# RWKV-7 in a hybrid encoder step: the output product in another PSUM pair, and the inverse's join issued earlier

## The chip, the cores and the metric

The kernel runs on one core of a Trainium2 chip. The metric is the device time of one execution in microseconds (us), the median of several executions. A profile is one further execution, taken with the hardware profiler; its span runs from the first to the last instruction. TensorE is called PE here (its weight loads PEld), VectorE DVE, ScalarE ACT, GpSimd POOL and SyncE SP.

## The reference, cut to what matters

One layer of a streaming encoder works on 1024 prompt frames and 32 sample frames. After a norm and one input projection, two groups of heads read the same rows: group A is sparse attention with a top-k choice of keys, group B is RWKV-7 time mixing. Their outputs go through one output projection, then a norm and a squared-ReLU feed-forward net. The change is in group B alone. There, for each of 8 heads, a 64 x 64 state S goes through the frames:

```python
def step(S, inp):
    r_t, w_t, k_t, v_t, kk_t, b_t = inp
    s_kk = jnp.einsum('bhvk,bhk->bhv', S, kk_t)
    S = S * w_t[:, :, None, :] - s_kk[..., None] * b_t[:, :, None, :] + v_t[..., None] * k_t[:, :, None, :]
    return S, jnp.einsum('bhvk,bhk->bhv', S, r_t)

s_fin, y = lax.scan(step, wkv0.astype(f32), (tm(r_h), tm(w_h), tm(k_h), tm(v_h), tm(kk), tm(kk * a_h)))
```

After it come a norm per head, a bonus term and a gate; the result has 512 columns per frame.

## The kernel before

The program has three stages. Stage one is the input projection and the choice of keys for the attention (`phase_a`). Stage two runs the attention (`attn_all`) and RWKV (`rwkv_all`) side by side. Stage three is the output projection (`project`, `project_early`) and the feed-forward net (`phase_c`).

**RWKV in units and chunks.** The 1056 frames are five units: 0 to 3 have 256 frames in four chunks of 64 (`NC = 4`, `w = 64`), unit 4 has the 32 sample frames in one chunk. A chunk is treated at once: with G, the masked products of keys, keys-times-a and receptances (L712, L715), the recurrence inside a chunk is a triangular system whose inverse is needed. Each unit goes through these steps:

- `rwkv_front` (L596): loads, decay and normalised keys (`head_stat` L790, `lora` L626, running sums L647, `head_bcast` L806), the tiles KB and AR (L681), and for each chunk G: 16 matmuls into two PSUM tiles (L712) and two masked copies on DVE (L715). Then `lane_inverse` (L810): four transposes on DVE (L824), 62 elementwise instructions on POOL one behind the other (L829, L831), and transposes back into G (L835) and X1 (L840) on DVE. This inverts the 32 x 32 diagonal blocks.
- `rwkv_join` (L757): combines two 32 x 32 inverses into the one of 64 x 64: 64 matmuls of 32 x 32 (L768), two ACT copies (L771), 64 matmuls (L776), two ACT copies (L779) into G. Only units with `w = 64` have it.
- `rwkv_tokens` (L736), for each chunk: 8 transposes of KB with two copies on ACT (L746, L747) and 4 of v with two copies (L750, L752): the chunk's keys and values by frame, in tiles KBs and VU with three buffers.
- `rwkv_back` (L843), the chain: for each chunk the product pR (L876, L880) is copied to rh (L882), pU (L888) is copied to VU (L889, L890), pS (L895) makes the next state (L901, L902), and the output product pY, 16 matmuls L906 and 16 matmuls L910, is copied to y by ACT (L911). The next chunk's pR needs the new state, not pY.
- `rwkv_norm` (L939): the norm of y, bonus and gate (`head_bcast` L806, L950, L790, L806, L968), and the store.

**PSUM.** There are eight banks. The names that matter: `pc`, one buffer, holds pR, pU, pS and pY one after the other, and both products of the join. `pr`, two buffers (`PRB`), holds the tiles of the front, the tokens and the norm, and those of `project_early` (L1256). The attention has `pd` (two), `ptr` (two) and `po` (one). A `pr` tile is given out when the tile two before it has been read; the tiles of a name are asked for in the order in which the program was written down.

**The order of the work.** The program is written down by generators: `rwkv_all` takes one step each from the back of unit i, the norm of unit i-1 and the front of unit i+2, in turn (`while gens`, L1018), and the body (L1498) takes a step of the attention, then a step of RWKV. Which instruction an engine takes next is settled at compile time by a planner: it plays the program against its own estimate of durations and takes, of what is ready, the one written down earliest, where `high_priority` moves a step's place: the back by +300 instructions (`BOFF`), the front by -100 (`FOFF`), all of RWKV by -200 (`OFF`). On the chip each engine then works its queue in that order.

**Around the change.** `rwkv_back` begins, at L854 to L858, with the tokens of chunks 0 and 1 where they are not there yet (unit 0 alone), and with the join of its own unit. In chunk c it writes down the tokens of chunk c+2 after pY; in chunks 2 and 3 these are the tokens of the next unit's chunks 0 and 1 (L914 to L917). `lane_inverse` of unit i+2 is written down after the chain of unit i.

Of the kernel before, what the change touches and what calls it, by code (L numbers as in the profile page):

```python
# [53 lines left out]
F32 = mybir.dt.float32  # L54
# [702 lines left out]
def rwkv_join(S, ps, U):  # L757

    nc = S.nc
    X1 = U.X1.rearrange("p (c h) t -> p c h t", c=4)  # L760

    def pc():
        return ps.tile([128, 512], F32, name="pc", bufs=1).rearrange("p (a b c) -> p a b c", a=4, b=4)
    p = pc()
    for cc in range(4):
        for hp in range(4):
            for par, b in ((0, 64), (1, 0)):
                nc.tensor.matmul(p[b + 32:b + 64, cc, hp], U.G[b:b + 32, par, cc, hp, 32:64], X1[b:b + 32, cc, hp],  # L768
                                 start=True, stop=True)
    for par, b in ((0, 64), (1, 0)):  # L770
        nc.scalar.copy(X1[b + 32:b + 64], p[b + 32:b + 64])  # L771
    p = pc()
    for cc in range(4):
        for hp in range(4):
            for par, b in ((0, 64), (1, 0)):
                nc.tensor.matmul(p[b:b + 32, cc, hp], X1[b + 32:b + 64, cc, hp], U.G[b + 32:b + 64, par, cc, hp, 32:64],  # L776
                                 start=True, stop=True)
    for par, b in ((0, 64), (1, 0)):
        nc.scalar.copy(U.G[b:b + 32, par, :, :, 32:64], p[b:b + 32])  # L779
# [63 lines left out]
def rwkv_back(S, rp, ps, U, state):  # L843
    nc, I, O = S.nc, S.I, S.O
    n, NC, w, u = U.n, U.NC, U.w, U.u
    G, AR = U.G, U.AR
    y = rp.tile([128, 4, 4, 64], F32, name="y", bufs=YB)

    def pc():
        return ps.tile([128, 512], F32, name="pc", bufs=1)  # L850

    def quarter(p):
        return p[:, 0:256].rearrange("p (a b) -> p a b", a=4)
    for c in range(len(U.tok), min(NC, 2)):  # L854
        U.tok.append(rwkv_tokens(S, rp, ps, U, c))
    tok = U.tok
    if w == 64:
        rwkv_join(S, ps, U)  # L858
    yield
    st = state.get("st")  # L860
    if u == 4:
        st = rp.tile([128, 4, 64], F32, name="st", bufs=3)
        si = S.rs.tile([64, 8, 64], F32, name="tmp", bufs=2)
        nc.sync.dma_start(si, I["state_wkv"][0, 0].rearrange("h v k -> v h k"))
        p = quarter(pc())
        for hp in range(4):
            nc.tensor.transpose(p[:, hp], si[:, 2 * hp:2 * hp + 2].rearrange("p a b -> p (a b)"), S.ident[0:64, 0:64])
        nc.scalar.copy(st, p)
    for c in range(NC):
        KBs, VU = tok[c]  # L870
        first = st is None
        pR = quarter(pc())
        pairs = [(hp, par) for hp in range(4) for par in range(2)]
        for hp, par in pairs:
            a, b = PAR[par], PAR[1 - par]
            nc.tensor.matmul(pR[b, hp], G[a, par, c, hp, 0:64], VU[a, par, hp], start=(hp == 0), stop=(first and hp == 3))  # L876
        if not first:
            for hp, par in pairs:
                a, b = PAR[par], PAR[1 - par]
                nc.tensor.matmul(pR[b, hp], AR[c][a, hp, 0], st[a, hp], start=False, stop=(hp == 3))  # L880
        rh = rp.tile([128, 4, 64], F32, name="rh", bufs=2)
        nc.vector.tensor_copy(rh, pR)  # L882
        yield
        pU = quarter(pc())
        for hp in range(4):
            for par in range(2):
                b = PAR[1 - par]
                nc.tensor.matmul(pU[b, hp], G[b, par, c, hp, 0:64], rh[b, hp], start=True, stop=True)  # L888
        nc.vector.tensor_copy(VU[64:128, 0], pU[64:128])  # L889
        nc.scalar.copy(VU[0:64, 1], pU[0:64])  # L890
        yield
        pS = quarter(pc())
        for hp in range(4):
            for par in range(2):
                nc.tensor.matmul(pS[PAR[par], hp], KBs[:, par, hp], VU[:, par, hp], start=True, stop=True)  # L895
        sn = rp.tile([128, 4, 64], F32, name="st", bufs=3)
        pcb = U.PC[:, c][:, :, None].to_broadcast([128, 4, 64])
        if first:
            nc.vector.tensor_tensor(sn, pS, pcb, op=ALU.mult)
        else:  # L900
            nc.vector.tensor_tensor(sn, pS, st, op=ALU.add)  # L901
            nc.vector.tensor_tensor(sn, sn, pcb, op=ALU.mult)  # L902
        yield
        pY = quarter(pc())
        for hp, par in pairs:
            nc.tensor.matmul(pY[PAR[par], hp], VU[:, par, hp], G[:, par, c, hp, 64:128], start=(hp == 0), stop=(first and hp == 3))  # L906
        if not first:
            for hp, par in pairs:
                a = PAR[par]
                nc.tensor.matmul(pY[a, hp], st[a, hp], AR[c][a, hp, 1], start=False, stop=(hp == 3))  # L910
        nc.scalar.copy(y[:, :, c], pY)  # L911
        st = sn
        U.done = c + 1
        if c + 2 < NC:  # L914
            tok.append(rwkv_tokens(S, rp, ps, U, c + 2))
        elif U.next and TOKN and len(U.next.tok) < U.next.NC:
            U.next.tok.append(rwkv_tokens(S, rp, ps, U.next, len(U.next.tok)))  # L917
        yield
    U.done = 4
    state["st"] = st  # L920
    if u >= 3:
        p = pc()[0:64].rearrange("p (a b c) -> p a b c", a=2, b=4)
        p2 = ps.tile([128, 512], F32, name="pr", bufs=PRB)[0:64].rearrange("p (a b c) -> p a b c", a=2, b=4)
        for hp in range(4):
            nc.tensor.transpose(p[:, 0, hp], st[0:64, hp], S.ident[0:64, 0:64])
        for hp in range(4):
            nc.tensor.transpose(p2[:, 1, hp], st[64:128, hp], S.ident[64:128, 64:128])
        so = S.rs.tile([64, 4, 2, 64], F32, name="tmp", bufs=2)
        nc.scalar.copy(so[:, :, 0], p[:, 0])
        nc.scalar.copy(so[:, :, 1], p2[:, 1])  # L930
        dst = O["wkv_prompt"] if u == 3 else O["wkv_sample"]
        nc.sync.dma_start(dst.rearrange("h v k -> v h k"), so.rearrange("p a b k -> p (a b) k"))
        if u == 3:
            state["st"] = None
    U.y = y
    yield
# [35 lines left out]


YB = 2


def rwkv_all(S, order):

    state = {"st": None}
    S.units = units = [K() for _ in order]  # L980
    fronts = []
    for i, U in enumerate(units):
        U.i, U.stage, U.tok = i, 0, []
        U.next = units[i + 1] if i + 1 < len(units) else None
        fronts.append(rwkv_front(S, order[i], U, units[i - 2] if i > 1 else None))

    def ahead(i):

        for _ in fronts[i]:
            if units[i].stage == 2 and i + 1 < len(order) and PRE and i >= PREI:  # L990
                break
            yield
        else:
            return
        yield
        for _ in range(PRE):
            next(fronts[i + 1])
            yield
        yield from fronts[i]

    def norm(i):
        if i >= 0:
            yield from rwkv_norm(S, S.P[0], S.ps, units[i])
        if 0 <= i + 2 < len(order):
            rwkv_prelude(S, S.P[0], units[i + 2])
    for i in range(-2, len(order) + 1):
        gens = []
        B = front = None
        if 0 <= i < len(order):
            B = units[i]  # L1010
            gens.append(back := rwkv_back(S, S.P[0], S.ps, B, state))
        if i >= -1:
            gens.append(norm(i - 1))
            if i == 0:
                shift_rows(S, S.P[0], S.ps)
        if i + 2 < len(order):
            gens.append(front := ahead(i + 2))
        while gens:  # L1018
            for g in list(gens):
                with S.tc.high_priority(BOFF) if B and g is back else S.tc.high_priority(F0 if i == -2 else F1 if i == -1 else FOFF) if g is front else nullcontext():  # L1020
                    if next(g, 1) == 1:
                        gens.remove(g)
                yield
# [348 lines left out]
PRB = 2  # L1372
# [38 lines left out]
def body(tc, I, O, dbg=None):  # L1411
# [4 lines left out]
    with pool(name="const") as cp, pool(name="dram", space=DRAM) as dp:  # L1416
# [18 lines left out]
        with pool(name="xnt") as xp, pool(name="psA", space=PSUM) as ps:  # L1435
# [27 lines left out]
            with pool(name="pq") as pq:  # L1463
                g = m3(pq, 4, 7)
                next(g)
                rwkv_setup(S)
                S.kv = {(0, False): attn_load(S, 0, False)}
                gr = rwkv_all(S, RORD)
                for _ in range(EARLYF):
                    next(gr)  # L1470
                for _ in g:
                    pass
# [65 lines left out]
```

## Time and profile before

| | |
|---|---|
| median of 3 executions | 1794.74 us (1794.37 to 1796.54) |
| the profiled execution | 1798.12 us, span 1796.3 us |
| PE busy | 1663.9 us (93%) |
| PEld busy | 1509.2 us (84%) |
| DVE busy | 936.1 us (52%) |
| ACT busy | 707.6 us (39%) |
| POOL busy | 618.6 us (34%) |

The shares are averages over the three stages. From about 420 to 933 us the attention and RWKV run side by side, before that is stage one, after it the output projection and the feed-forward net, in which PE is busy nearly throughout. PE has two clock levels; the profile gives the granted clock as a share of the higher one, so 0.5 is 1.2 GHz and 1.0 is 2.4 GHz. A busy PE is not PE at its peak, as matmuls are pipelined.

### The profile page before, as it was taken

What the parts mean: (1) busy time and instruction counts of PE and PEld (TensorE: products, weight loads), DVE (VectorE), ACT (ScalarE), POOL (GpSimd) and SP (SyncE); (2) the same over time, 40 slices, a digit from 0 to 9 for tenths busy, and PEclk for the clock granted to TensorE, in tenths of its full rate; (3) what the DMA queues carried; (4) which work ended last, traced back from release to release, by engine and by line L of the source; (5) the groups of instructions that cost most, each with busy time, mean ns of one, the idle gap of its engine ahead of it and who ended that gap; (6) DMA issues with size and microseconds to landing.
All of it is one profiled execution on the core that took longest, in us unless ns stands there. A gap on an engine that the chain in (4) does not pass through costs nothing.

```text
span 1796.3 us, 30013 instructions
## 1 busy us (share of the span) xinstructions
PE 1663.9 (93%) x11686; PEld 1509.2 (84%) x11686; DVE 936.1 (52%) x1996; ACT 707.6 (39%) x1549; POOL 618.6 (34%) x919
## 2 busy tenths in 40 slices
PE   7999979986569898999899999999999999999999
PEld 6787779986456777767678799999999999999998
DVE  6477889975878687577562533222222222222224
ACT  6365667897446344344641331222222121212120
POOL 7468863353543443056210021222222222222120
PEclk9999989996559697798899999999999999999999
DMA  7211131323110202140323341111111111111105
GB/s 218 54 36 43 42 88 64 110 68 92 29 27 14 40 24 57 26 101 17 98 76 123 121 125 49 46 48 45 49 37 53 42 53 42 47 44 51 36 16 172
DMA packets 180775, 113.25 MB, mean 63 GB/s; under 512 B 51969, under 2 KB 169817, under 8 KB 180633
## 3 DMA queue, kind: packets, MB, share of 16 engines
q1 hardware_dynamic: 171800, 107.00, 21.4%
q10 hardware_dynamic: 8832, 4.33, 0.9%
q8 instruction: 92, 1.51, 0.4%
q14 instruction: 51, 0.41, 0.1%
HBM read 86.29 MB, written 25.01 MB: 62 GB/s over the span
## 4 chain that ended last, share of the span: by engine, by line
PE 63%; DVE 12%; ACT 5%; POOL 4%; issue 3%; DMA 2%; SPq 0%; DVEq 0%; ACTq 0%; POOLq 0%
PE pd L1320 20%; PE pr L1340 10%; PE pc L1340 5%; PE po L1340 5%; PE pd L1256 3%; PE po L1139 2%; DVE AR L342 2%; ACT AR L362 2%; PE ptr L1123 2%; PE pr L1256 2%; PE acc L440 2%; DVE L L824 1%; PE pr L712 1%; POOL tl L829 1%; POOL Yl L831 1%
## 5 line engine op out<-in xcount | busy, mean ns | idle before, releaser
L1320 PE MATMUL pd<-hh,w1h 128*128 128x352 f32 x768 | 248.6, 324 | 2.2 <-issue 1.4
L1320 PE MATMUL pd<-hh,w1l 128*128 128x352 f32 x768 | 248.2, 323 | 0.7 <-DVE w1l L1187 0.7
L1320 PE MATMUL pd<-hl,w1h 128*128 128x352 f32 x768 | 247.5, 322 | 0.0
L1326 DVE TENSOR_TENSOR h2l<-rl,h2h 128x352 fp32r<-128x352 f32 x96 | 56.9, 592 | 277.3 <-ACT h2h L1325 277.3
L1324 POOL TENSOR_TENSOR rl<-rl 128x352 f32<-128x352 f32 x96 | 85.2, 888 | 215.5 <-ACT rl L1323 215.5
L1186 ACT CAST w2h<-w2r 128x512 fp32r<-128x512 f32 x64 | 39.7, 621 | 293.0 <-PE po L1340 144.8
L1320 PEld LDWEIGHTS pd<-hh,w1h 128*128 128x128 f32 x768 | 144.7, 188 | 2.8 <-issue 1.7
L1320 PEld LDWEIGHTS pd<-hh,w1l 128*128 128x128 f32 x768 | 144.8, 189 | 0.9 <-DVE w1l L1187 0.9
L1320 PEld LDWEIGHTS pd<-hl,w1h 128*128 128x128 f32 x768 | 145.3, 189 | 0.0
L1187 POOL TENSOR_TENSOR w2l<-w2r,w2h 128x512 fp32r<-128x512 f32 x32 | 41.6, 1299 | 299.3 <-ACT w2h L1186 288.8
L1340 PE MATMUL pr<-h2h,w2l 128*128 128x352 f32 x384 | 124.3, 324 | 0.0
L1340 PE MATMUL pr<-h2h,w2h 128*128 128x352 f32 x384 | 124.3, 324 | 0.0
L1340 PE MATMUL pr<-h2l,w2h 128*128 128x352 f32 x384 | 124.1, 323 | 0.0
L362 ACT ACTIVATE AR<-G,cnd 128x768 bf16<-128x768 f32 (+2 forms) x93 | 96.7, 1040 | 42.2 <-DVE cnd L367 36.8
L1323 ACT ACTIVATE rl<-pd 128x352 f32<-128x352 f32 x96 | 44.3, 463 | 143.4 <-PE pd L1320 136.9
L1346 DVE TENSOR_TENSOR ya<-ya,pr 128x352 f32<-128x352 f32 x84 | 43.8, 521 | 101.0 <-PE pr L1340 101.0
L829 POOL TENSOR_TENSOR tl<-L,Yl 128x56 f32<-128x56 f32 (+22 forms) x155 | 65.9, 425 | 60.5 <-DVE L L824 50.0
L1105 ACT ACTIVATE s<-s,m 32x544 f32<-32x544 f32 (+8 forms) x72 | 55.4, 770 | 74.8 <-DVE m L1102 74.6
L1123 PE MATMUL ptr<-ident,s 128*128 128x128 f32 (+2 forms) x328 | 69.4, 321 | 16.2 <-ACT s L1105 11.2
L1325 ACT CAST h2h<-rl 128x352 fp32r<-128x352 f32 x96 | 46.6, 485 | 75.3 <-POOL rl L1324 75.3
L1340 PEld LDWEIGHTS pr<-h2l,w2h 128*128 128x128 f32 x384 | 72.3, 188 | 0.1
L1340 PEld LDWEIGHTS pr<-h2h,w2h 128*128 128x128 f32 x384 | 72.2, 188 | 0.1
(443 smaller groups left out, 4655.1 us busy)
## 6 DMA issues: line engine op xcount, KB each, us to landing
w1r<-in_w_ff_dram SPq DMA_DIRECT2D x32, 512.0 KB, 4.1
w2r<-in_w_ff_dram SPq DMA_DIRECT2D x64, 256.0 KB, 2.9
zsd<-zm SPq DMA_DIRECT2D x12, 528.0 KB, 2.7
wraw<-in_w_in_dram SPq DMA_DIRECT2D x24, 256.0 KB, 2.7
wraw<-in_w_in_dram SPq DMA_DIRECT2D x40, 128.0 KB, 2.2
x<-in_x_prompt_dram SPq DMA_DIRECT2D x8, 512.0 KB, 5.0
hres<-hd ACTq DMA_DIRECT2D x16, 256.0 KB, 3.3
out_dram<-hres SPq DMA_DIRECT2D x16, 256.0 KB, 2.3
```

Of the source, the lines that this page charges most:

```text
L362: nc.scalar.activation(junk2[:r, :n], S.sc[t][:r, :n], AF.Sign, bias=c_of(j, r), scale=-1.0, accum_out=cnt[:r, j:j + 1])
L829: eng.tensor_tensor(t_, L[:, 0:j, j:j + 1].to_broadcast([128, j, w]), Y[:, j:j + 1, m:16].to_broadcast([128, j, w]), op=ALU.mult)
L1105: nc.scalar.activation(s, s, AF.Exp, bias=m[:, i:i + 1], scale=-1.0, accum_out=w.m[:, 6 + h:7 + h])
L1123: nc.tensor.transpose(p[:x, i, h, :r], w.s[h][:, c0 + i * 128:c0 + i * 128 + x], S.ident[:r, :r])
L1256: nc.tensor.matmul(acc[:r], a[:, k], b, start=(i == 0), stop=(i == 23))
L1320: nc.tensor.matmul(acc, a[:, k], m[:, k, o:o + n], start=(i == 0), stop=(i == 23))
L1323: nc.scalar.activation(rl, acc, AF.Relu)
L1324: nc.gpsimd.tensor_tensor(rl, rl, rl, op=ALU.mult)
L1325: nc.scalar.copy(h2h[:, o:o + n], rl)
L1326: nc.vector.tensor_tensor(h2l[:, o:o + n], rl, h2h[:, o:o + n].bitcast(F32), op=ALU.subtract)
L1340: nc.tensor.matmul(acc, a[:, k], m[:, o:o + n], start=(i == 0), stop=(i == 11))
L1346: nc.vector.tensor_tensor(y, y, acc, op=ALU.add)
```

## The change

The output product pY and both products of the join take their PSUM tiles from `pr` in place of `pc`. The join of the next unit is written down in chunk 2 of the running unit's chain, after pY and ahead of the next unit's first tokens, no longer at the head of the next chain. For unit 0, which has no chain before it, a new generator `first` writes down the tokens of chunks 0 and 1 and then, `JOIN0` = 4 steps later, the join, beside the front of unit 1; before, they stood at the head of unit 0's chain, behind that front.

```diff
@@ rwkv_join
     def pc():
-        return ps.tile([128, 512], F32, name="pc", bufs=1).rearrange("p (a b c) -> p a b c", a=4, b=4)
+        return ps.tile([128, 512], F32, name="pr", bufs=PRB).rearrange("p (a b c) -> p a b c", a=4, b=4)
@@ rwkv_back
     for c in range(len(U.tok), min(NC, 2)):
         U.tok.append(rwkv_tokens(S, rp, ps, U, c))
     tok = U.tok
-    if w == 64:
-        rwkv_join(S, ps, U)
     yield
...
-        pY = quarter(pc())
+        pY = quarter(ps.tile([128, 512], F32, name="pr", bufs=PRB))
...
         U.done = c + 1
+        if U.next and c == 2 and U.next.w == 64:
+            rwkv_join(S, ps, U.next)
         if c + 2 < NC:
             tok.append(rwkv_tokens(S, rp, ps, U, c + 2))
@@ rwkv_all
+JOIN0 = 4
...
+    def first():
+
+        U = units[0]
+        for c in range(2):
+            U.tok.append(rwkv_tokens(S, S.P[0], S.ps, U, c))
+            yield
+        for _ in range(JOIN0):
+            yield
+        rwkv_join(S, S.ps, U)
+        yield
+
...
             gens.append(norm(i - 1))
+            if i == -1:
+                gens.append(first())
```

## Rows read from the trace of the kernel before

**Rows 1.** Busy time by stretch: start:end, length, PE, PEld, DVE, ACT, POOL, PEclk.
```profile
460.00:520.00 60.00, 27.13 (x129) 18.86 (x127) 51.93 (x101) 21.63 (x52) 38.69 (x68) 0.53 0.14 25
...
540.00:933.00 393.00, 361.04 (x3935) 281.31 (x3933) 275.69 (x639) 185.68 (x461) 148.38 (x315) 0.85 0.20 48
...
840.00:933.00 93.00, 85.70 (x1003) 66.39 (x1002) 61.34 (x172) 51.38 (x128) 29.93 (x47) 0.93 0.26 72
```

**Rows 2.** What PE waited for from 540 to 933 us: total, times, longest.
```profile
PE ptr L1123 <- ACT s L1105: 6.7, 6, 2.2
PE pr L746 <- DVE G L715: 4.9, 2, 4.0
...
PE pc L906 <- DVE st L899: 1.5, 1, 1.5
PE pc L876 <- ACT G L779: 1.3, 1, 1.3
```

**Rows 3.** PE's timeline around unit 0's join, front of unit 1 and first tokens.
```profile
521.87 1.91 PE L768 MATMUL pc<-X,G 32*32 32x32 f32 x62 [2.12 <-DVE m L1109]
...
541.05 0.48 PE L626 MATMUL pr<-wa,w 96*128 96x256 f32 x2
...
557.40 1.16 PE L712 MATMUL pr<-AR,KB 64*128 64x128 f32 x8
...
558.87 0.27 PE L115 MATMUL pr<-ident,shl 128*28 128x128 f32 x1
...
560.30 0.46 PE L746 MATMUL pr<-ident,KB 64*128 64x64 f32 x4
...
568.28 0.33 PE L876 MATMUL pc<-VU,G 64*64 64x64 f32 x2
```

**Rows 4.** Busy PE and PEld by stretch, for L746, L750, L768 (two rows) and L776 alone.
```profile
560.00:574.00 14.00, 2.06 (x16) 1.47 (x16) 0.88 0.04 12
...
560.00:574.00 14.00, 1.66 (x8) 1.13 (x8) 0.88 0.04 12
...
517.00:532.00 15.00, 2.23 (x64) 1.96 (x64) 0.50 0.36 60
643.00:650.00 7.00, 1.20 (x64) 1.09 (x64) 1.00 0.34 93
...
517.00:532.00 15.00, 1.92 (x64) 1.79 (x64) 0.50 0.36 60
```

**Rows 5.** Timelines of ACT and PE where one unit's chain ends and the next begins.
```profile
641.70 0.35 ACT L911 COPY y<-pc 128x256 f32<-128x256 f32 x1
...
644.90 1.17 ACT L771 COPY X<-pc 32x512 f32<-32x512 f32 x2
...
650.35 0.68 PE L876 MATMUL pc<-VU,G 64*64 64x64 f32 x16 [1.26 <-ACT G L779]
...
731.48 0.37 ACT L911 COPY y<-pc 128x256 f32<-128x256 f32 x1 [0.97 <-PE pc L910]
...
747.90 1.12 PE L876 MATMUL pc<-VU,G 64*64 64x64 f32 x16
```

**Rows 6.** PE's timeline: first and last pr tiles of one round, norm and tokens in unit 2.
```profile
642.33 1.16 PE L712 MATMUL pr<-AR,KB 64*128 64x128 f32 x16
...
754.49 0.79 PE L712 MATMUL pr<-AR,KB 64*128 64x128 f32 x2
...
765.41 0.68 PE L910 MATMUL pc<-AR,st 64*64 64x64 f32 x16
...
778.86 1.99 PE L968 MATMUL pr<-zg,g 96*128 96x256 f32 x8
...
783.32 0.47 PE L746 MATMUL pr<-ident,KB 64*128 64x64 f32 x8
```

**Rows 7.** PE's timeline where the stage ends.
```profile
930.61 0.33 PE L1143 MATMUL po<-ident,x 128*128 128x128 f32 x1
...
931.93 1.08 PE L968 MATMUL pr<-zg,g 96*128 96x32 f32 x8 [0.63 <-DVE y L961]
933.03 0.49 PE L1256 MATMUL pr<-G 128*128 128x512 f32 x1
```

## The prediction

> **What bounds the kernel now.** I read the busy time by stretch first. Between 540 and 933 us, where attention and RWKV run side by side, PE is busy 361.0 of 393 us, at a mean granted clock of 0.85; between 460 and 520 us it is busy only 27.1 of 60 us, at 0.53 [rows 1]. So in the first stretch PE, in its given order, is nearly full, and 32 us of idle time are all that a change without fewer matmuls can take out of it; in the second there are 33 us of room. Second, the list of what PE waited for in the full stretch: the longest is the attention's own (6.7 us, transposes waiting for ACT's exponentials); of RWKV's, 4.9 us are tokens waiting for the masked copies of G, and two that the change touches are 1.5 us (pY waiting until DVE has read pS out of the single `pc`) and 1.3 us (the chain waiting for the join's last copies) [rows 2]. Third, the end: the attention's last matmul starts at 930.61, RWKV's last product at 931.93, and the output projection, whose tiles stand behind RWKV's in `pr`, at 933.03 [rows 7]. Both strands end together; speeding up one of them moves the end only through the PE time it leaves to the other.
>
> **An order that matters.** Unit 0's join and its first tokens are written down at the same place. The join, first in `pc`, ran at 521.87, as soon as the inverse allowed. The tokens ran at 560.30, behind the last G product of unit 1 (557.40) and the shift transpose (558.87), which stand before them in `pr`, and unit 0's chain began at 568.28 [rows 3]. So the tiles of `pr` come strictly in written order, and moving work into `pr` puts it into that line.
>
> **Part by part.**
>
> *First tokens early.* They need KB and v of unit 0; G of unit 0, made from the same KB, is written down ahead of them, and their new place in `pr` is right behind it, around the key broadcast of unit 1: they move from the full stretch to the one with room. They cost PE 2.06 + 1.66 = 3.7 us at 560 to 574 [rows 4]. Nothing else moves with them but eight ACT copies: no DMA, nothing on SP or POOL. ACT is busy 21.6 of 60 us there [rows 1], which hides the copies; without that cover they would add eight times 0.35 to 0.37 us, some 3 us (ACT's 256-column copy y [rows 5]). Bounds -3.7 and +3; I take **-3.7**, as PE's and ACT's room is in the row.
>
> *First join.* It leaves 517 to 532, where its matmuls take 2.23 + 1.92 us at clock 0.50 [rows 4]. In `pr` it stands behind the decay products of unit 2 (541.05) and G of two chunks of unit 1 [rows 3], so it runs at about 548 to 554, later than before, at the price of unit 1's join, 1.20 us a half at clock 1.00 [rows 4]. Bounds: 2.4 - 4.15 = -1.8 where the old place was full, +2.4 where it had room. I take **-1**, nearer the first, as PE's waits there are short (2.12 us ahead of the join itself [rows 3]). The chain of unit 0 then starts at about 555 in place of 568. Between its halves lie ACT copies of 1.17 us, and both its tiles are in `pr`: G of unit 1's chunks 2 and 3, queued behind, and so unit 1's inverse, come some 5 us later. That is hidden: unit 1's chain started at 650.35, and moved by the 13 us that unit 0 starts sooner it would start at 637 [rows 5]. Were unit 0's chain much faster, the 5 us would count.
>
> *pY out of `pc`.* The next pR no longer waits for 32 output matmuls and y's copy. PE's work is the same; what it gives PE directly is the 1.5 us wait [rows 2]. *The next unit's join inside the chain* takes two copies and 128 matmuls out of the way from one unit to the next: y to pR took 8.65 us (641.70 to 650.35) and 16.42 us (731.48 to 747.90) [rows 5]; PE's wait there is 1.3 us [rows 2]. Bounds: 0 (other waits take their place) and -2.8; I take **-2.8**, since nothing else stood in `pc`.
>
> *A wait that is added.* The join in chunk 2 needs the next unit's inverse, and PE takes its queue in order, so the attention stands behind it. Unit 0's join shows the size: 2.12 us [rows 3]. Units 1 to 3 could each pay that, 0 to 6.4 us; I take one, **+2.1**, for unit 1, whose inverse comes 5 us later while the chain ahead of it comes 13 us sooner. In `pr`, the next tokens, pY of chunk 3 and the remaining G products queue behind the join; they run beside attention work.
>
> *The end.* With RWKV ending earlier, the projection fills PE's holes beside the last attention items. From 840 to 933 these are 93 - 85.7 = 7.3 us [rows 1]. Bounds 0 and -7.3; I take **-1.5**, a fifth, as most of the stretch lies before the attention's first tiles of the last head are stored.
>
> The eight extra steps of `first` also put RWKV eight attention steps further back in the written order; as attention fills what RWKV leaves, I count 0 (with that cover gone, a step's wait of 1 to 2 us).
>
> Sum: -3.7 - 1 - 2.8 + 2.1 - 1.5 = -6.9 us. It is made against the profiled execution (1798.12 us, of it 1796.3 the span), which lies 3.4 us above the median of 1794.74; on the median it gives **1788 us**. Its own range by the bounds is 1780 to 1793.
>
> **Rivals.**
>
> *The freed bank buys nothing* (0.20). PE is 92% busy in the stretch, and the waits named are replaced by others of the same queue. For it: the attention's waits alone (6.7 us) exceed those removed [rows 2]. Against it: the tokens really leave. It gives 1793 to 1796, say 1794.5. The Trainium skill, "TensorE: Matmul & The Clock Gate", section "HAM oscillation — how this bites in real kernels", tells of a kernel in which adding PSUM double-buffering gave no further gain; by it my 2.8 us would go and the sum be -4.1.
>
> *Slower: `pr` becomes the bound* (0.20). Place: the two `pr` buffers. Each unit puts up to six more tiles into a line that already sets part of the chain: tokens of unit 2's third chunk came only at 783.32, behind the norm's last product at 778.86 [rows 6], and pR needs them. From one last G product to the next (642.33 to 755.28) 37 tiles passed (by the code 9 of the norm, 16 of the front, 12 of tokens), 3.05 us each [rows 6]. Six more cost at most 18 us a unit, and at least four times 0.9 (32 matmuls 1.36, copy 0.35, over two buffers [rows 5, 6]) plus 4.7 for the join's two halves and copies [rows 4, 5], 8.3 us. It decides from the point where the line, not `pc`, makes the chain wait, that is where the gain of 6 to 14 us between units is smaller than this. Over 3.3 units the least is 27 us; RWKV then ends after the attention, and with PE half filled in that tail about 13 us are lost; less the tokens' 3.7: about 1804 (1799 to 1812).
>
> *Much faster: the chain, not PE, is the bound* (0.15). If PE's busy time hides room, the gaps between units, 8.65 and 16.42 shrunk to 2 each, move the stage's end by 21 us: 1774 (1768 to 1780). For it: PEld is busy only 281 of 393 us [rows 1]. Against it: the attention ends no sooner by that. The Trainium skill, "Perfetto Trace Analysis", section "Identifying the Most-Contended Engine", says that matmul busy time is no good measure of the distance to the roofline and weight-load busy time is; the row's 72% agrees that there is room, and no row tells whether this order can use it.
>
> The granted clock goes with all of these: at 0.85 over 393 us, a change of 0.01 is some 4 us where PE is the bound, and which stretches fall to 1.2 GHz I can't tell from rows.
>
> **How the numbers follow.** Forecast 0.45, the freed bank 0.20, `pr` 0.20, the chain 0.15. A measurement tells about 0.2%, 3.6 us, from no change. Below 1791.1: four fifths of the forecast and the last rival, 0.51; within: the rest of the forecast and most of the first rival, 0.28; above: 0.21. The range 1775 to 1805 leaves out about half of each outer rival.
>
> **What would show it.** Right: L746 and L750 of unit 0 before 480; the first L768 at 545 to 555; no L779 between the last L911 of a unit and the next L876, and that gap at 2 to 5 us; RWKV's last L968 before 925; PE busy at over 93% until the projection. Wrong: PE idle ahead of L768 in units 1 to 3 of more than 2 us each; tokens or G later in each unit than before; the last L968 after 935; or a mean clock in 540 to 933 that differs from 0.85 by more than 0.03, which would outweigh the sum.

## The result, and the profile after

The changed kernel takes **1814.32 us** (median of 4 executions, 1809.97 to 1818.76), the kernel before in the same comparison 1794.55 us: a ratio of **1.0107**, 95% interval 1.0081 to 1.0133. It is 1.1% slower; forecast were 1788 us and a range of 1775 to 1805. The profiled execution took 1818.76 us, its span is 1817.0.

The page of the changed kernel: busy time of the engines, and the granted clock in 40 slices of the span:

```profile
PE 1688.4 (93%) x11686; PEld 1522.9 (84%) x11686; DVE 938.6 (52%) x1996; ACT 709.4 (39%) x1549; POOL 621.5 (34%) x919
...
PEclk9999989996559587588989999999999999999999
```

The same stretches as in [rows 1], after:

```profile
460.00:520.00 60.00, 29.66 (x152) 21.20 (x152) 51.22 (x98) 21.36 (x53) 37.66 (x68) 0.50 0.15 28
540.00:933.00 393.00, 371.73 (x3894) 286.58 (x3893) 264.40 (x604) 180.50 (x439) 149.69 (x313) 0.81 0.17 44
840.00:933.00 93.00, 87.84 (x1025) 68.37 (x1026) 60.90 (x157) 50.78 (x127) 42.96 (x84) 0.92 0.19 56
```

Between 540 and 933 PE is idle for 21.3 us, 10.7 less than before, and still gets through fewer matmuls, 3894 in place of 3935: one takes on average 371.73 / 3894 = 95 ns of busy time in place of 92, at a mean clock of 0.81 in place of 0.85. What was not done by 933 follows after it. The end of the stage (PE's timeline, to be read beside [rows 7]):

```profile
946.01 0.33 PE L1158 MATMUL po<-ident,x 128*128 128x128 f32 x1
...
950.48 1.91 PE L968 MATMUL pr<-zg,g 96*128 96x32 f32 x8 [0.28 <-DVE y L961]
952.20 0.77 PE L1271 MATMUL pr<-G 128*128 128x512 f32 x1
```

The projection starts at 952.20 in place of 933.03, 19.2 us later; the span is 20.7 us longer. RWKV ends last; before, both strands ended within 1.3 us of each other.

What PE waited for from 540 to 933 (beside [rows 2]): the tokens' wait for G, 4.9 us, is gone, and what is left at pY (0.6 us, 1.5 before) and at pR (1.6 us, 2.1 before on its two lines) is shorter. Some waits, most of them the attention's, are new or longer, none by more than 2.7 us. Nothing in the list is of the size of the delay.

```profile
PE ptr L1138 <- ACT s L1120: 3.9, 5, 1.9
PE ptr L1079 <- DVE ph L1139: 2.7, 1, 2.7
...
PE pc L878 <- DVE st L900: 1.6, 1, 1.6
...
PE pr L904 <- DVE VU L887: 0.6, 1, 0.6
```

So the order has to be read, from the timeline. Unit 0's tokens, join and first pU on PE (beside [rows 3]):

```profile
458.20 0.69 PE L746 MATMUL pr<-ident,KB 64*128 64x64 f32 x4
...
470.91 1.06 PE L750 MATMUL pr<-ident,v 128*64 128x128 f32 x4
...
545.56 0.57 PE L768 MATMUL pr<-X,G 32*32 32x32 f32 x24
...
550.76 0.24 PE L768 MATMUL pr<-X,G 32*32 32x32 f32 x2
552.78 0.24 PE L776 MATMUL pr<-G,X 32*32 32x32 f32 x2
...
562.81 0.43 PE L776 MATMUL pr<-G,X 32*32 32x32 f32 x14
...
566.61 0.33 PE L886 MATMUL pc<-rh,G 64*64 64x64 f32 x2
```

The tokens are done by 472, as meant. The join, 64 matmuls a half, is torn into pieces between other work, 17.7 us from first to last; pU, which needs it, comes at 566.61. Further on, PE from the last chunk of unit 0 into unit 1:

```profile
618.20 1.12 PE L904 MATMUL pr<-G,VU 128*64 128x64 f32 x16
...
624.32 1.20 PE L768 MATMUL pr<-X,G 32*32 32x32 f32 x64
628.12 1.92 PE L776 MATMUL pr<-G,X 32*32 32x32 f32 x64
629.97 0.69 PE L746 MATMUL pr<-ident,KB 64*128 64x64 f32 x4
...
649.97 0.64 PE L904 MATMUL pr<-G,VU 128*64 128x64 f32 x16
...
660.19 0.48 PE L712 MATMUL pr<-AR,KB 64*128 64x128 f32 x2
...
688.84 1.10 PE L968 MATMUL pr<-zg,g 96*128 96x256 f32 x4
...
693.18 0.69 PE L904 MATMUL pr<-G,VU 128*64 128x64 f32 x16
...
696.17 0.46 PE L746 MATMUL pr<-ident,KB 64*128 64x64 f32 x4
```

Line by line: pY of unit 0's chunk 2 (618.20), unit 1's join, tokens, G, and only then pY of unit 0's last chunk (649.97), all tiles of `pr` in written order; then the last G of unit 2 (660.19). The norm of unit 0, which needs that pY, ends at 689.9; pY of unit 1's chunk 0 stands behind it (693.18), and the tokens of unit 1's chunk 2 behind that (696.17). Before, the copy of these tokens into VU began at 686.3, now at 698.6.

### The profile page after: what moved, and what is told of

Same layout as the page of the kernel before. It is cut to its first block, busy times and chain, and to the rows that moved or that the text cites. A ratio compares the mean times of both kernels' runs of the same rounds, so it can differ in the third digit from the quotient of the medians.

```text
span 1817.0 us, 30033 instructions
## 1 busy us (share of the span) xinstructions
PE 1688.4 (93%) x11686; PEld 1522.9 (84%) x11686; DVE 938.6 (52%) x1996; ACT 709.4 (39%) x1549; POOL 621.5 (34%) x919
## 4 chain that ended last, share of the span: by engine, by line
PE 62%; DVE 14%; ACT 5%; issue 3%; POOL 3%; DMA 2%; SPq 0%; ACTq 0%; DVEq 0%; POOLq 0%
PE pd L1335 19%; PE pr L1355 10%; PE pc L1355 5%; PE po L1355 5%; PE pd L1271 3%; DVE AR L342 3%; PE pr L1271 2%; ACT AR L362 2%; PE po L1154 2%; DVE L L824 2%; PE ptr L1138 2%; PE pr L712 2%; PE pd L1114 1%; DVE cnd L367 1%; DVE G L835 1%
## 5 line engine op out<-in xcount | busy, mean ns | idle before, releaser
L1138 PE MATMUL ptr<-ident,s 128*128 128x128 f32 (+2 forms) x328 | 70.1, 321 | 23.3 <-ACT s L1120 15.6
L1138 PEld LDWEIGHTS ptr<-ident,s 128*128 128x128 f32 (+2 forms) x328 | 42.9, 163 | 40.0 <-ACT s L1120 20.1
L831 POOL TENSOR_TENSOR Yl<-Yl,tl 128x56 f32<-128x56 f32 (+22 forms) x155 | 69.1, 446 | 10.9
```

What stands on the lines that cost most here:

```text
L831: eng.tensor_tensor(Y[:, 0:j, m:16], Y[:, 0:j, m:16], t_, op=ALU.add)
L1138: nc.tensor.transpose(p[:x, i, h, :r], w.s[h][:, c0 + i * 128:c0 + i * 128 + x], S.ident[:r, :r])
```

## The experiments

Each kernel was timed in 4 rounds against the kernel before (its medians 1795.7 to 1796.5 us). Two more numbers of the profiled execution stand with most of them: when the norm of unit 0 has its last product (L968 of the kernel before; "norm 0") and when RWKV has its last one ("end"). Before they are 682 and 933, after 690 and 952.

### The parts alone, and pY taken back

**a1** is the change with pY again in `pc`; **b1** is the kernel before with pY alone in `pr`.

```diff
-        pY = quarter(pc())
+        pY = quarter(ps.tile([128, 512], F32, name="pr", bufs=PRB))
```

> The changed kernel with the output product pY back in pc (join in pr, join in the chain and early first unit stay). Theory P (the line of pr tiles is longer and sets the chain): four of the six added pr tiles a unit are gone, so at least half of the 20 us loss returns, 1795 to 1804 us, and unit 1's third-chunk tokens come before 690 us instead of 696. Theory C (the loss is time at the 1.2 GHz level, 160 us instead of 123 after 538 us, whatever made the order): the time follows the half-clock time, about half a microsecond for each, and pY's place by itself says nothing; if the long half-clock stretch at 705 to 770 stays, the time stays at 1808 to 1818.

> The kernel before with only pY moved to pr. Theory P: slower by 6 to 15 us, 1800 to 1810, with third-chunk tokens of units 1 and 2 later than 684 and 783 us. Theory C: time follows the half-clock time after 538 us (123 us before); with the join where it was I expect the same clock and 1790 to 1797 us.

a1: 1839.78 us, 1.022 (1.0184 to 1.0257), norm 0 at 694, end 979, above both ranges: taking pY back makes the change worse by 25 us. b1: 1817.07, 1.0121 (1.0077 to 1.0165), norm 0 at 696, end 949: alone it loses 21 us, more than theory P has. So the same edit costs or gains, by its company.

**b2**: the kernel before with the next unit's join in chunk 2, still in `pc`. **b3**: the kernel before with unit 0's tokens alone early.

```diff
 # b2, in rwkv_back; unit 0's join stays at the head
-    if w == 64:
+    if w == 64 and U.i == 0:
         rwkv_join(S, ps, U)
...
         U.done = c + 1
+        if U.next and c == 2 and U.next.w == 64:
+            rwkv_join(S, ps, U.next)
 # b3, in rwkv_all, beside norm(-1)
+    def first():
+        U = units[0]
+        for c in range(2):
+            U.tok.append(rwkv_tokens(S, S.P[0], S.ps, U, c))
+            yield
```

> The kernel before with only the next unit's join written down in chunk 2 of the running chain, its tiles still in pc (unit 0's join stays at the head of its chain). Theory P: no added pr tile, so no loss: 1785 to 1796 us, the gap from y to the next unit's pR shrinks. Theory C: if the join's 32x32 matmuls amid the chain's small ones keep the clock at 1.2 GHz, the loss appears here: over 1803 us with over 140 us of half clock after 538 us.

> The kernel before with only unit 0's tokens of chunks 0 and 1 written down early (its join stays in pc at the head of the chain, so that it runs at about 520 us). Both theories: the part of my forecast that should hold, -3.7 us of PE time and unit 0's chain from 568 us to about 535 us: 1783 to 1793 us. If it is slower than 1797, the chain's earlier start itself costs, and neither pr nor the join's place is the cause.

b2: 1800.28, 1.0016 (0.9998 to 1.0034), norm 0 at 691, between its two ranges. b3: 1781.71, **0.99** (0.9863 to 0.9937), norm 0 at 662, end 919. With the tokens early and the join where it was, unit 0's chain begins at 532 in place of 568: the early tokens came with nearly four times the 3.7 us that they free on PE (what of it goes with the clock stands further down).

### The join's bank

**c1**: the change with pY and all joins in `pc`. **c2**: the kernel before with the joins' tiles in `pr`, written at the head of the chain as before.

```diff
 # c2, in rwkv_join
-        return ps.tile([128, 512], F32, name="pc", bufs=1).rearrange("p (a b c) -> p a b c", a=4, b=4)
+        return ps.tile([128, 512], F32, name="pr", bufs=PRB).rearrange("p (a b c) -> p a b c", a=4, b=4)
```

> The changed kernel with both its moves to pr undone: pY and the joins take pc again, the early tokens, the early first join and the join in the chain stay. If the loss is pr's alone, this is the sum of the two parts that were run alone, -14 us (tokens early) and +4.5 us (join in the chain): 1782 to 1790 us, with unit 0's join done by 532 us. If the early writing-down of the first join costs by itself, it stays over 1795 us.

> The kernel before with only the joins' two tiles in pr, at the head of each chain as before. If a join costs by its place in the pr line: unit 0's join moves from 520 to behind unit 1's G, to about 560 us, beside tokens that ran there anyway, and the later joins stand behind the front's tiles, so 1798 to 1812 us. If pY is all of the loss: 1792 to 1799 us.

c1: 1810.59, 1.0084 (1.0062 to 1.0106). c2: 1775.68, **0.9895** (0.9872 to 0.9919), norm 0 at 681, end 909. c1 came out on the second branch of its expectation, by which the early first join costs by itself: with `pc` the change is still slow. c2 missed both of its branches: one line of the change, by itself, is faster than both kernels. PE of c2 at the first boundary between units (beside [rows 5]):

```profile
642.62 0.68 PE L876 MATMUL pc<-VU,G 64*64 64x64 f32 x16
...
645.95 1.20 PE L768 MATMUL pr<-X,G 32*32 32x32 f32 x64
649.65 1.20 PE L776 MATMUL pr<-G,X 32*32 32x32 f32 x64 [0.16 <-DVE G L715]
652.46 0.68 PE L888 MATMUL pc<-rh,G 64*64 64x64 f32 x16
```

pR does not need the join, only pU does. With `pc` free, pR goes ahead of the join and pU comes straight behind it; in the kernel before pR had to wait until 650.35 [rows 5], and pU came at 659.20:

```profile
659.20 0.68 PE L888 MATMUL pc<-rh,G 64*64 64x64 f32 x16
```

### Is it the number of tiles in `pr`, or what they wait for?

**d1** adds to the kernel before, right behind pY, one tile of `pr` with one matmul and a copy of four columns that nothing uses; its matmul reads a constant. In **d2** that matmul reads VU and G, as pY does. The computation is otherwise the same.

```diff
+        pD = ps.tile([128, 512], F32, name="pr", bufs=PRB)
+        nc.tensor.matmul(pD[0:64, 0:64], S.ident[:, 0:64], S.ident[:, 0:64], start=True, stop=True)     # d1
+        nc.tensor.matmul(pD[0:64, 0:64], VU[:, 0, 0], G[:, 0, c, 0, 64:128], start=True, stop=True)     # d2
+        dd = rp.tile([128, 4], F32, name="dd", bufs=2)
+        nc.scalar.copy(dd[0:64], pD[0:64, 0:4])
```

> The kernel before, pY in pc, with one more pr tile at pY's place in each chunk: one 64-column matmul of a constant and a copy of 4 columns that nobody reads, 17 in all, ready at any time. If the length of the pr line is the cost (theory L), it costs 1 to 1.5 us a tile while RWKV sets the end: 1803 to 1818 us. If the cost is that a pr tile is held back until the chain has its data and all behind it wait (theory H), it is free but for its 17 small matmuls: 1793 to 1800 us.

> As the run with the empty tile, but its one matmul reads the chunk's VU and G, as pY does, so that the tile can be filled only when the chain is there. Theory H: most of the loss of pY in pr (21 us alone) shows with a 32nd of its matmuls, 1805 to 1820 us, and the tokens of unit 1's third chunk come after 690 us. Theory L: the same time as the empty tile, within 4 us. If both are below 1799, neither, and pY's loss is its leaving pc.

d1: 1789.14, the median of ten executions (one more, of 4133.31 us, is left out), 0.9963 (0.9927 to 0.9999), norm 0 at 684. d2: 1820.51, 1.0149 (1.0122 to 1.0177), norm 0 at 689, end 963. The same number of tiles in the line, a difference of 1.9%. It stands at an equal clock too: where the granted clock was 0.927, d1 took 1797.3 and 1798.78 us, d2 1816.01 and 1819.95. A place in `pr` costs next to nothing (at this clock 17 of them 1 to 3 us); a place whose contents come late costs, as every tile written behind it waits too.

### Together, and reordered

**e1**: b3 with the joins of units 1 to 3 in `pr` at the head, unit 0's in `pc`. **e2**: b1, **e3**: the change, both with the tokens of chunk c + 2 written ahead of pY of chunk c. **e4**: the change with unit 0's join in `pc`.

```diff
 # e1, e4, in rwkv_join
+        return ps.tile([128, 512], F32, name="pr" if U.i else "pc", bufs=PRB if U.i else 1).rearrange("p (a b c) -> p a b c", a=4, b=4)
 # e2, e3, in rwkv_back
+        if c + 2 < NC:
+            tok.append(rwkv_tokens(S, rp, ps, U, c + 2))
...
         pY = quarter(ps.tile([128, 512], F32, name="pr", bufs=PRB))
```

> The kernel before with the two parts that helped alone: unit 0's tokens early, and the joins of units 1 to 3 in pr at the head of their chains (unit 0's join stays in pc, where it runs at about 520 us). Compared at the same time at 1.2 GHz, the tokens were worth -3 us and the joins in pr -7 us. If the parts add: 1766 to 1780 us, faster than both kernels. If the gains were the clock's by chance (its runs differ by 20 us within one program), no better than the parts alone: 1775 to 1796 us.

> The kernel before with pY in pr as in the run of that part alone (1817 us), but with the chunk's tokens written down ahead of pY, so that they no longer stand behind it in the pr line. Theory H (tokens and all behind wait until the chain fills pY's tile): most of the 21 us goes, 1792 to 1803 us, and unit 1's third-chunk tokens come before 692 us. If pY in pr costs in another way (its leaving pc lets the planner bunch the chain's small matmuls, and the clock falls): still 1808 to 1820 us.

> The changed kernel whole, with the chunk's tokens written down ahead of pY and of the next unit's join. Theory H: 1790 to 1803 us in place of 1814, with RWKV's last product before 940 us. If the early first join or the join in the chain is the cause: 1808 to 1820 us.

> The changed kernel with unit 0's join alone back in pc (it no longer stands behind unit 1's G in the pr line, so it can run at about 520 us instead of 545 to 563). If the late first join costs the gain of the early tokens: 1800 to 1809 us, with unit 0's first pU before 545 us. If pY in pr is nearly all of the loss: 1810 to 1820 us.

e1: 1783.39, 0.9929 (0.9917 to 0.9942), norm 0 at 674, end 910. It beats both kernels, but the two gains don't add. e2: 1806.21, 1.0042 (1.0021 to 1.0063), between its two ranges: of b1's 1.21% two thirds are gone, so pY's hold on the tokens was part of it. e3: 1809.27, 1.0059 (1.0041 to 1.0077): in the whole change the same order gives back 5 us; the hold by pY is not its main cause. e4: 1803.15, 1.0036 (1.0024 to 1.0049): unit 0's join in `pr` costs the change 11 us. The time is that of e4's first branch, the sign that was to go with it isn't: the first pU came at 558.37, not before 545.

### The parts added to e1, one at a time

**f1**: e1 with pY in `pr` (as b1). **f2**: e1 with the joins of units 1 to 3 in chunk 2 (as b2, but in `pr`). **f3**: f1 with the tokens ahead of pY (as e2). **f4**: b3 and c2 together.

> The early tokens and the joins of units 1 to 3 in `pr` (1783.4) with pY's tile in `pr` besides; the joins stay at the head of the chain. If pY in `pr` costs here what it cost alone (1817.1 against 1796, some 20 us), 1800 to 1806: then it is the part that turns the change's sign. If its price comes only together with a join in chunk 2, or was paid already by the joins in the same line, 1780 to 1790.

> The same start with the next unit's join in chunk 2 of the chain and in `pr`; pY stays in `pc`. If the parts add, the 4 us that this place cost with the join in `pc` come on top: 1785 to 1790. If a join in `pr` between two chunks holds the tokens behind it as pY does (which would explain why writing the tokens ahead of pY alone didn't mend the change), 1797 to 1806.

> The first of these runs with the tokens of chunk c + 2 written ahead of pY of chunk c. If pY's price is that its tile holds the tokens behind it, most of what the first loses against 1783.4 comes back: 1783 to 1792. If the tokens are late for another reason in this company (pY itself then waits behind them and holds the norm), it stays at the first's time, above 1797.

> The two parts that made the kernel faster, together and whole: unit 0's tokens early, all four joins in `pr` at the head of their chains (1781.7 and 1775.7 alone). If they add at an equal clock, -3.7 and -7.5 of 1796 give 1785, and by what each measured, clock included, 1761 to 1770. If they don't add, because unit 0's join in `pr` comes behind unit 1's G and takes the early tokens' gain back, 1776 to 1786, no better than the joins alone.

f1: 1775.42, **0.9894** (0.987 to 0.9919), norm 0 at 666, end 909, below both ranges: pY in `pr` costs nothing here. f2: 1814.32, 1.0108 (1.0094 to 1.0123), norm 0 at 688, end 947, above both: the join's place alone takes 31 us, and ends at the time of the whole change. f3: 1783.98, 0.9939 (0.9921 to 0.9956), 9 us above f1: here the order only costs. f4: 1778.69, 0.991 (0.9894 to 0.9925), norm 0 at 671, on its second branch.

Why f2 loses is in its trace. PE around unit 1's join:

```profile
606.78 1.16 PE L712 MATMUL pr<-AR,KB 64*128 64x128 f32 x8
...
624.34 1.92 PE L768 MATMUL pr<-X,G 32*32 32x32 f32 x64
...
629.23 1.50 PE L776 MATMUL pr<-G,X 32*32 32x32 f32 x64
630.65 0.47 PE L746 MATMUL pr<-ident,KB 64*128 64x64 f32 x4
...
648.06 1.16 PE L712 MATMUL pr<-AR,KB 64*128 64x128 f32 x16
```

and DVE, where unit 1's inverse is turned back:

```profile
617.11 4.55 DVE L835 STREAM_TRANSPOSE G<-Yl 32x512 f32<-32x512 f32 x4 [0.83 <-POOL Yl L831]
...
622.69 1.43 DVE L840 STREAM_TRANSPOSE X<-G 32x512 f32<-32x512 f32 x2
```

From 607.94 to 624.34 no matmul enters a `pr` tile: the join holds the line for 16.4 us until the inverse is through. Tokens and G stand behind it, as 630.65 and 648.06 show; in e1 this stretch holds tokens (609.0) and G. PE's list of waits can't show this, for PE works on the attention meanwhile. In the change itself the line doesn't stand like this: between 611 and 625 it takes G and pY, and its join (624.32) follows on a G product that ends at 624.39. No stretch of over 6 us without a matmul into `pr` stands ahead of a join there.

### The join's two moves within the change

**g1**: the change with the joins of units 1 to 3 back at the head of their chains (in `pr`); it differs from f1 only in unit 0's join (its place behind the tokens and `JOIN0` steps, and its bank). **g2**: the change with the next unit's join in chunk 3, behind the tokens.

```diff
 # g1
+    if w == 64 and U.i:
+        rwkv_join(S, ps, U)
...
-        if U.next and c == 2 and U.next.w == 64:
-            rwkv_join(S, ps, U.next)
 # g2: the same two lines, with c == 3, behind the tokens
```

> The whole change but for one part: the joins of units 1 to 3 stand at the head of their own chains, as before, with their tiles in `pr`; tokens of unit 0 early, its join early, pY in `pr`. If the join inside the running chain is what turned the change's sign (there its tile stands in `pr` waiting for the next unit's inverse while nothing else enters the line), 1775 to 1786. If pY's tile or the early first join carries the loss, it stays near the change: above 1800.

> The whole change with the next unit's join one chunk later and behind that chunk's tokens, still inside the running chain. If the hold of `pr` is the cost, a later place, when the inverse is done or nearly done, sheds most of it: 1776 to 1795. If being inside the running chain costs in itself (the join's matmuls and copies ahead of the last chunk, or PE's order), 1800 to 1816.

g1: 1824.85, 1.0173 (1.0141 to 1.0204), norm 0 at 687, end 963. g2: 1825.73, 1.0177 (1.0159 to 1.0195), norm 0 at 691, end 967. Both expected numbers of the hold missed (g1 is on its second branch, g2 above both): with the join taken out of the chain the change is no faster. Against f1, the move of unit 0's join, place and bank together, costs 49 us. The bank alone is not it, at least with pY in `pc`: e1 to f4, which moves unit 0's join into `pr` at the head of its chain, costs nothing (1783.39 to 1778.69). PE of f1:

```profile
523.26 1.91 PE L768 MATMUL pc<-X,G 32*32 32x32 f32 x62 [2.12 <-DVE m L1118]
529.62 1.20 PE L776 MATMUL pc<-G,X 32*32 32x32 f32 x64
533.92 1.12 PE L876 MATMUL pc<-VU,G 64*64 64x64 f32 x16
546.98 0.68 PE L876 MATMUL pc<-VU,G 64*64 64x64 f32 x16
...
623.03 1.12 PE L906 MATMUL pr<-G,VU 128*64 128x64 f32 x16
...
630.29 1.16 PE L712 MATMUL pr<-AR,KB 64*128 64x128 f32 x8
...
664.61 1.03 PE L968 MATMUL pr<-zg,g 96*128 96x256 f32 x4
...
670.37 1.12 PE L906 MATMUL pr<-G,VU 128*64 128x64 f32 x16
672.06 0.46 PE L746 MATMUL pr<-ident,KB 64*128 64x64 f32 x4
```

In `pc` the join is through at 531, and the chain's second chunk starts at 546.98, when the change's join has only just begun (545.56). pY of the last chunk of unit 0 is at 623.03 in f1, and at 649.97 after; the norm ends at 665.6 and 689.9; the tokens of unit 1's chunk 2 are at 672.06 and 696.17. The same three steps follow one another at the same distances, 24 to 27 us later.

That the chain starts late isn't enough for this, as f4 shows. PE of f4:

```profile
553.62 1.20 PE L768 MATMUL pr<-X,G 32*32 32x32 f32 x64
...
562.10 0.33 PE L888 MATMUL pc<-rh,G 64*64 64x64 f32 x2
...
625.12 0.94 PE L712 MATMUL pr<-AR,KB 64*128 64x128 f32 x12
...
669.53 1.03 PE L968 MATMUL pr<-zg,g 96*128 96x256 f32 x4
```

Its first pU (562.10) comes 4.5 us ahead of that of the change (566.61) and 23.5 us behind that of f1 (538.64), and still its norm 0 ends at 671 and it takes 1778.69 us. By unit 0's last chunk little is left of the head start: pU is at 603.69 in f1, 612.34 in f4, 614.80 in g1 and 614.22 after. What goes with norm 0 in all 20 traces is the last G product of unit 2, which stands ahead of the norm in `pr`: it ends at 626 in f4, 631 in f1, 643 before, 649 in f2, 650 in g1 and 661 after, and norm 0 ends 29 to 45 us behind it. Each G of unit 2 is written down only behind the same chunk of unit 0. pY's late place (649.97) is not needed for the delay: in a1 and f2, with pY in `pc`, unit 0's last pY is done by 631 and 612, and norm 0 ends at 694 and 688.

## Why the prediction was wrong

**The sum.** From f1 to the change there are two steps, both of the join: unit 0's into the early place and into `pr`, the others' into chunk 2. Either is enough: f1 to g1 +49 us, e1 to f2 +31 us. Together they make +39 (f1 to the change): in the presence of the first the second gains 10 (g1 to the change). By their times the early tokens gain, and the joins in `pr` at the head gain. That each of the join's moves turns the sign in its company is shown; that their prices don't add is measured and not explained. The prediction's own range is also added up wrongly: its bounds run from -15.6 to +11.8 us, 1779 to 1807 us, and not 1780 to 1793. The measured 1814 us lies outside that too.

**First tokens early**: the place and the time of the work were right (458 to 472). b3 measured -14 us, not -3.7. What the move buys besides PE time is a chain that begins 36 us sooner; the change gives most of that back, since its join comes at 546. But nearly all of b3's 14 us go with its higher clock (see below), so the -3.7 is neither refuted nor shown.

**First join (-1)** is the first step that failed. "At about 548 to 554" was near for its begin (545.56); the price taken from unit 1's join, 1.20 us a half, was not. Its two halves, L768 and then L776, were busy for 2.05 and 2.42 us, more than the 4.15 us of the old place that they were to save:

```profile
545.00:564.00 19.00, 2.05 (x64) 1.49 (x64) 1.00 0.05 13
...
545.00:564.00 19.00, 2.42 (x64) 1.64 (x64) 1.00 0.05 13
```

And they are spread over 17.7 us, with pU at 566.6 where the text has the chain at 555. The comparison was made with the 568 of the kernel before. But the tokens, which held the chain until 568, leave in the same change; by the time that they leave, the old join at 523 to 531 is the one that counts, and against it the first pU comes 28 us later (538.6 in f1, 566.6 after). The step was measured at +49 us (f1 to g1) in place of -1. How it costs that stays open: of the 28 us 10.5 are left by unit 0's last chunk, and f4, nearly as late at first, is fast. The section on the kernel before says that the back is moved up by 300 instructions in the planner's order; `first` has no such line. The bank is not why the join is torn: c1 and e4, with the early join in `pc`, have it drawn out from 518 (516) to 547, and f4, with the join in `pr` at the head of the chain, has its first half in one piece (553.62). That it is the missing 300 instructions is argued, not tried alone.

**pY out of `pc`, the join inside the chain (-2.8, "bounds: 0 and -2.8")** is the second. No loss was let in as a bound. "Nothing else stood in `pc`" looks at what a tile leaves; what it enters, the line of `pr`, was not priced. The join in chunk 2 is worth +31 us (e1 to f2), and in f2 it holds the line for 16.4 us. pY is worth +21 us alone, -8 in f1, and -25 in the change: of no sign of its own.

**The added wait (+2.1, 0 to 6.4)**: the wait for the inverse was looked for on PE. There the change shows 0.3 us ahead of L768 in units 1 to 3. In f2 it is paid in the line of `pr`, as PE has other work meanwhile; in the change it is paid in neither.

**The end (-1.5)** became +19: the projection starts that much later, with RWKV last.

**The rivals.** "Slower: `pr` becomes the bound" (0.20, 1799 to 1812) had the place, the third chunk's tokens behind the norm, and nearly the size. Its price, at least 0.9 and up to 3.05 us for every tile in the line, is refuted by d1: a tile that fills at once costs next to nothing. "Much faster" (0.15, 1774) wasn't this change, yet c2 and f1 reach its time. The first part of the prediction says that the 32 us of idle time in the full stretch are all there is to win; c2 shows otherwise. From 540 to 933 in c2:

```profile
540.00:933.00 393.00, 363.22 (x4133) 286.83 (x4131) 278.49 (x635) 189.58 (x463) 149.84 (x314) 0.90 0.22 57
```

These are 198 matmuls more than in [rows 1], in 2 us more of busy time, at a clock of 0.90 in place of 0.85. Of the two pages cited, the Trainium skill's "Perfetto Trace Analysis" (section "Identifying the Most-Contended Engine"), by which busy matmul time is no good measure of the distance to the roofline, agrees with this row, though the clock has a part in it. The example in the Trainium skill's "TensorE: Matmul & The Clock Gate" (section "HAM oscillation — how this bites in real kernels"), where PSUM double-buffering brought nothing, doesn't carry over: c2 moves the join from the one buffer of `pc` to the two of `pr` and gains 1.05%.

**The clock**: the text says that a mean clock off by over 0.03 would outweigh the sum; it was 0.81, off by 0.04. d1 gives its price, as one program came out in two groups: five executions of 1774.57 to 1780.98 us at mean clocks of 0.937 to 0.942, five of 1797.3 to 1800.59 at 0.922 to 0.927, some 20 us for 0.015. By it, an estimate, the step from 0.927 (the mean over the executions before) to 0.9205 (the change) is some 8 of the 20 us. The same estimate gives the clock 25 of the 49 us from f1 to g1 (mean clocks 0.940 and 0.920), 18 of the 31 from e1 to f2 (0.930 and 0.916), 12 of c2's 21 (0.937) and 13 to 14 of b3's 14 (0.9365). The signs of the first three stand without it, at half the size or less; b3's gain doesn't. Whether the lower clock is a consequence of the order or only came with it stays open.

**The signs to look for**: tokens before 480, the join at 545, PE over 93% busy (371.7 of 393) came true and said nothing of the sign. The gap from y to the next pR is gone altogether, as unit 1's first pR (638.51) runs ahead of unit 0's last pY (649.97); that said nothing either. Of the signs of being wrong, PE idle ahead of L768 didn't come. The last L968 (950.5, set were 925 and 935), later tokens from unit 1 on and the clock were the ones that told.

One sign would have sorted all 20 kernels better than any sum. Norm 0 ends by 675 us in b3, e1, f1, f3 and f4: all faster, 1775 to 1784. It ends from 686 on in a1, b1, b2, c1, d2, e3, e4, f2, g1, g2 and the change: none faster, 1800 to 1840. From 681 to 685 lie c2, d1, e2 and the kernel before, of both signs (the profiled executions of d1 and e2, 1779.3 and 1791.11 us, are among the fastest of theirs).

**What stays open**: how unit 0's early join costs 49 us, why the join's two moves cost no more together than the first alone, why pY's price changes sign with its company, and how much of each difference is the clock. b3 with the early join added and nothing else, and f4 with pY in `pr`, were not tried. Six versions clearly beat both kernels (b3, c2, e1, f1, f3, f4); the fastest two can't be told apart: c2, one line (1775.68), and f1 (1775.42).

## What to carry to other kernels

When a tile is moved to another PSUM name, price the line that it enters: who stands behind it, and how late what fills it can be; a tile tied to a late producer stops the line (d2, f2), an extra one that fills at once costs next to nothing (d1). Such a hold needn't show in a list of an engine's waits, as the engine finds other work; look for the stretch in which no tile of that name is filled. Where there is none, as in the change, follow the order of the tiles up to the first one that comes later than in a faster version. And price the parts of a change against each other and not each against the kernel before: a part that removes one limit makes the next one, which another part may be moving, the one that counts.

## What was not expected of the hardware

The same program (d1), run after run on one chip, came out in two groups some 20 us apart, with the mean granted clock as the only difference that the results show. And PE's busy time grew by 24.5 us (1663.9 to 1688.4) with the same 11686 matmuls: busy time has to be read beside the granted clock of its stretch.
